# Scores of both attentions: the rounded queries meet the rest of the keys in two 64-row matmuls, one per half of the array

## The chip, the cores and the metric

The kernel runs on one core of one Trainium2 chip. The metric is the time of one execution in microseconds (us), as a median over runs. TensorE (PE) multiplies, VectorE (DVE) and ScalarE (ACT) take its results out of PSUM and round them, GpSimd (POOL) does a few small sums, SyncE (SP) issues the transfers. Each engine works through its own list in order.

## The reference, cut to what matters

One decoder block over 1024 positions, all in float32: a SwiGLU half-step, a mixer of two attentions, a cross attention over 256 memory rows, a second SwiGLU half-step, a final norm. The change is in the mixer's two attentions:

```python
qg = q.reshape(b, s, G, J, D) * (D ** -0.5)          # NSA: 8 heads of width 64, in 2 key groups
s_c = einsum(qg, kc) + bias_c                         # scores against 63 compressed keys
sc  = einsum(qb, kg) + bias                           # against the selected blocks of keys
s_w = einsum(qw, kwin) + bias_w                       # against a window of 512 keys
...
sc = jnp.einsum('bhqd,bkhd->bhqk', qi, k).astype(jnp.float32) + ci[..., None] - c[:, :, None, :]   # FoX: 8 heads
p = masked_softmax(sc, mask)
```

With 16 blocks of 64 keys and top 16 of them, the selection keeps every block up to the query's own, so that the kernel computes it as plain causal attention.

## The kernel before, in words

Matmuls take fp32r operands, which are rounded. To keep float32's precision, each operand is split into a rounded value ("hi") and the rest that rounding left ("lo"). Scores have a contraction of only 64 (the head's width), half of the array's 128 rows, and the kernel uses the other half for the split: a query tile `Q[e]` has the rounded queries in 64 of its rows and their rest in the other 64; a key tile `K1` has the rounded keys twice, one above the other, and `K2` has the rest of the keys twice. So `Q` by `K1` gives (hi + lo) by the rounded keys in one 128-row matmul, and `Q` by `K2` gives (hi + lo) by the rest of the keys in another, accumulated in the same PSUM bank.

`group` (line 1142) does one row of blocks: two heads `e` of NSA for one block of 128 queries, or two neighbouring blocks of queries of one head of FoX. `nb[e]` is the number of 128-key blocks that a row needs. A row that is too wide for one bank of 512 columns is cut into two pieces. For each `e` and each piece, one operation on PE, `scores`, takes a PSUM bank of the tag `s` and issues the matmul by `K1` (line 1167), the one by `K2` (line 1168) and, in the last piece of a window row, one by the 63 compressed keys in plain float32 (line 1170), which the hardware does as two. The weights of all of these, the stationary operand, are the 128 columns of `Q[e]`. Behind them DVE adds bias and mask and takes the minimum (lines 1178, 1265), ACT takes the exponential (line 1195), DVE or ACT scales (1209, 1211), PE transposes the probabilities into tag `T` (line 388), ACT and DVE split them (397, 404), and PE multiplies by the values into tag `pv` (line 1242).

`attention` calls `group` 16 times for each of 4 pairs of NSA heads (8 blocks of queries, each once for the selection and once for the window with the compressed keys) and 4 times for each of 8 FoX heads. Beside these run the projections of the FoX queries, keys and values and of the gates (`proj`, `mm3`, lines 382 to 384, matmuls of 512 columns). `load_q` (line 666) fills `Q` for NSA from DRAM, `proj_q` (line 1075) fills it for FoX from a projection's bank; both write the rounded value and the rest with one ACT and one DVE operation for each `e` and half. `hi_at` says in which 64 rows the rounded queries stand.

The order on every engine is written ahead by a planner (`Plan.order`), a list scheduler with a cost in ns for each operation; it hands out the 8 banks of PSUM, with a cap for each tag (`s` 3, `T` 2, `pv` 1, `mm` 3). An operation on PE gets its banks when it is placed.

Earlier, at line 988, one small product stands in the first SwiGLU: the table of relative biases, a plain float32 matmul with a contraction of 32 and a stationary operand of 8 columns. It is the only place of the kernel where a matmul uses fewer than 128 rows of the array.

Of the kernel before, what the change touches and what calls it, by code (L numbers as in the profile page):

```python
# [10 lines left out]
F32 = mybir.dt.float32  # L11
F32R = mybir.dt.float32r
BF16 = mybir.dt.bfloat16
AF = mybir.ActivationFunctionType
# [5 lines left out]
P = 128  # L20
# [141 lines left out]
class Plan:  # L162
# [120 lines left out]
}  # L283
# [3 lines left out]
class Halves:  # L287
# [13 lines left out]
    def at(self, hf, k, a=0, b=512):  # L301
        return [self.t[hf][s][k // 2]()[:, (k % 2) * 512 + a:(k % 2) * 512 + b] for s in range(2)]
# [19 lines left out]
class Block:  # L322
# [37 lines left out]
    def pe(self, ns, run, reads, writes):  # L360
        self.plan.op({"PE": ns}, lambda _: run(), reads, writes, self.r)
        self.r += ns * self.rate / 1000
# [300 lines left out]
            self.split(1024, lambda raw=raw: [raw()], lambda e=e: [K1[e]()], lambda e=e: [K2[e]()], [raw], [K1[e]], [K2[e]],  # L663
                       rank=r, sbuf=True)

    def load_q(self, name, Q, hi_at, lead=14.0):

        nc = self.nc
        for e in range(2):
            raw, r = self.load_rows(name, e, lead)  # L670
            lo = slice(64 - hi_at[e], 128 - hi_at[e])
            self.act(1024, lambda raw=raw, e=e: nc.scalar.activation(Q[e](), raw(), AF.Copy, scale=-0.125), [raw], [Q[e]],
                     sbuf=True, rank=r)
            self.dve(1135, lambda raw=raw, e=e, lo=lo: nc.vector.scalar_tensor_tensor(
                Q[e]()[lo, :], raw()[lo, :], -0.125, Q[e]()[lo, :].bitcast(F32), op0=ALU.mult, op1=ALU.subtract),
                [raw], [Q[e]], rank=r)
# [395 lines left out]
        self.cd = self.dram([8, S], "cd")  # L1072
        self.dma(32768, lambda: nc.sync.dma_start(self.cd().rearrange("h (b p) -> (h b) p", p=P), ct()[0:64, 0:P]), [ct], [self.cd])

    def proj_q(self, key, hT, Q, hi_at, **k):

        def evac(hf, ps):
            sl = slice(hf * 512, hf * 512 + 512)
            for e in range(2):
                h0 = hi_at[e]  # L1080
                self.split(512, lambda e=e: [ps()[64 * e:64 * e + 64, :]], lambda e=e, h0=h0: [Q[e]()[h0:h0 + 64, sl]],
                           lambda e=e, h0=h0: [Q[e]()[64 - h0:128 - h0, sl]], [ps], [(Q[e], hf)], [(Q[e], hf)], scale=-0.125)
        self.proj(key, hT, evac, **k)

    def proj_k(self, key, hT, K1, K2, **k):
# [56 lines left out]
    def group(self, kind, i, nb, r, Q, K1, K2, V, bias, out, unit, last=True, k0=0, mask=None, cmp=None, gate=None):  # L1142
        nc = self.nc
        mm = nc.tensor.matmul
        rank = self.r
        pe = lambda ns, run, reads, writes: self.plan.op({"PE": ns}, lambda _: run(), reads, writes, rank)
        keys = lambda bs, b: [(x, h) for x in bs for h in range((b + 3) // 4)]
        p, m, l = [self.buf("p") for _ in range(2)], [self.buf("sm") for _ in range(2)], self.buf("sm")
        total = 0.0
        row = [nb[e] * P for e in range(2)]  # L1150
        z = lambda e: p[e]()[:, 896:960]
        for e in range(2):
            n = nb[e]
            if n <= (3 if cmp else 4):
                pieces = [(0, n)]
            else:
                a = min(4, n - 2)
                pieces = [(0, a), (a, n - a)]
            for j, (b, w) in enumerate(pieces):
                end = j == len(pieces) - 1  # L1160
                st = self.buf("s")

                def scores(e=e, b=b, w=w, end=end, st=st):
                    q = Q[e]()[:, i[e] * P:(i[e] + 1) * P]
                    c = max(2, w) * P
                    ks = slice((k0 + b) * P, (k0 + b) * P + c)
                    mm(st()[:, 0:c], q, K1()[:, ks], start=True, stop=False)  # L1167
                    mm(st()[:, 0:c], q, K2()[:, ks], start=False, stop=True)  # L1168
                    if cmp and end:
                        mm(st()[:, 448:512], q.bitcast(F32), cmp[0](), start=True, stop=True)  # L1170
                ns = 2 * max(w * P, 256) / 2.4 + 27 + (110 if cmp and end else 0)
                total += ns
                pe(ns, scores, keys([K1, K2], k0 + b + max(2, w)) + [(Q[e], i[e] // 4)] + ([cmp[0]] if cmp else []), [st])

                if mask is not None and (end if kind == "fox" else j == 0):
                    def masked(w=w, st=st):
                        d = st()[:, w * P - P:w * P] if kind == "fox" else st()[:, 0:P]
                        nc.vector.tensor_add(d, d, mask)
                    self.dve(200, masked, [], [st], rank)

                def biased(e=e, b=b, w=w, j=j, st=st):
                    at = b * P if kind == "fox" else S - row[e] + b * P
                    self.ttr_min(p[e]()[:, b * P:(b + w) * P], st()[:, 0:w * P], bias[e]()[:, at:at + w * P],
                                 m[e]()[:, j - 1:j] if j else 3.0e38, m[e]()[:, j:j + 1])
                self.dve(1.042 * w * P + 74, biased, [bias[e], st] + ([(m[e], j - 1)] if j else []), [(p[e], j), (m[e], j)], rank)
                if end and cmp:
                    def blocks(e=e, st=st):
                        w0 = e * P + 56 - 8 * i[e]
                        self.ttr_min(z(e), st()[:, 448:512], cmp[1]()[:, w0:w0 + 64], 3.0e38, m[e]()[:, 2:3])
                    self.dve(143, blocks, [cmp[1], st], [(p[e], "z"), (m[e], 2)], rank)  # L1190

                    self.pool(90, lambda e=e: nc.gpsimd.memset(p[e]()[:, 960:1024], 0.0), [(m[e], 2)], [(p[e], "end")], rank)

            def exps(e=e, j=len(pieces) - 1):
                nc.scalar.activation(p[e]()[:, 0:row[e]], p[e]()[:, 0:row[e]], AF.Exp, bias=m[e]()[:, j:j + 1], scale=-1.0,  # L1195
                                     accum_out=l()[:, e:e + 1])
                if cmp:
                    nc.scalar.activation(z(e), z(e), AF.Exp, bias=m[e]()[:, 2:3], scale=-1.0, accum_out=l()[:, 2 + e:3 + e])
            self.act(row[e] + (220 if cmp else 70), exps, [m[e]], [p[e], (l, e)], count=4 if cmp else 2, sbuf=True, acc=2 if cmp else 1,
                     table="exp", rank=rank)  # L1200

        k = 4 if cmp else 2
        self.dve(100, lambda: nc.vector.reciprocal(l()[:, 0:k], l()[:, 0:k]), [], [l], rank)
# [14 lines left out]
        n = max(nb)  # L1218
# [57 lines left out]
    def attention(self, hT, kcs, Q, K, V):  # L1276
# [10 lines left out]
        def fox_set(j):  # L1287
            s = dict(Q=u("Q"), K1=u("K1"), K2=u("K2"), V=u("V"))
            return s, [lambda: self.proj_k(("kf", j), hT, s["K1"], s["K2"]), lambda: self.proj_v(("vf", j), hT, s["V"]),
                       lambda: self.proj_q(("qf", j), hT, s["Q"], (0, 64))]  # L1290

        def finish(c, oc):
            if c == 7:
# [6 lines left out]
        for c in range(4):  # L1300
            r0 = self.r
            bias, be = [self.buf("b") for _ in range(2)], self.buf("be")
            self.r = r0 - 6
            self.bias_tile(c, bias, be)
            if c < 3:
                Qn, h0, work = u("Q"), 64 * ((c + 1) // 2), []
                self.r = r0 + 45.0
                self.load_q(("qn", c + 1), Qn, (h0, h0))
                self.r = r0
            else:  # L1310
                fox, work = fox_set(0)
            work += gate(GATES[c])
            r1 = r0 + 51.0 + 10.9 * len(work)
            self.r, self.rate = r0, (r1 - r0) / 51.0
            oc, g, h = self.buf("oc"), c // 2, 2 * c
            for i in range(NT):
                k0, unit = max(0, i - 4), {}
                com = dict(kind="nsa", i=(i, i), r=64 * g, Q=Q, unit=unit, bias=bias, out=(oc, i))
                self.group(nb=(i + 1, i + 1), K1=K[0][0][g], K2=K[0][1][g], V=V[0][g], last=False,
                           gate=lambda i=i, h=h: self.gate()[:, i, 8 + h:10 + h], **com)  # L1320
                self.group(nb=(i + 1 - k0,) * 2, K1=K[1][0][g], K2=K[1][1][g], V=V[1][g], k0=k0, mask=self.win if i >= 4 else None,
                           cmp=(kcs[0][g], be, kcs[1][g]),
                           gate=lambda i=i, h=h: self.gate()[:, i, :].rearrange("p (k h) -> p k h", h=8)[:, 2::-2, h:h + 2], **com)
            self.rate = 1.0
            finish(c, oc)
            self.side(r0, r1, work)
            if c < 3:
                Q = Qn
# [210 lines left out]
    def run(self):  # L1539
# [64 lines left out]
        chains[1]()  # L1604
        for n, k in zip(("ks", "kw"), K):
            self.load_k((n, 0), *k)
        self.load_q(("qn", 0), Q, (0, 0))
        for _ in range(G0):
            self.proj_gate(self.gates.pop(0), hT2)
        self.attention(hT2, self.compressed, Q, K, V)  # L1610
# [28 lines left out]
MLATE = {3: 14.0, 4: 18.0, 1: 24.0, 6: 28.0, 7: 32.0}  # L1639
FIRST = 2  # L1640
G0, AHEAD, MAHEAD, NB = 0, 2, 2, 0
LATER = {4: 8.0, 2: 11.0, 1: 14.0, 6: 17.0, 7: 20.0}


# [20 lines left out]
```

## Time and profile before

| | us |
|---|---|
| median of 3 runs (2528.48 to 2533.14) | 2530.29 |
| the profiled execution | 2531.05 |
| its span, first to last instruction | 2529.3 |
| PE busy | 2497.9 |
| DVE busy | 1777.8 |
| ACT busy | 1201.9 |

How to read it: a matmul's end is modelled and lies well after the start of the next one, since matmuls are pipelined. What a matmul costs PE is therefore read from the distance of two starts. PEld is the load of a matmul's weights into the array, which can run beside the matmul before it. The scores lie between 874 and 1506 us of the span.

### The profile page before, as it was taken

The numbers are of one execution on the slowest core, as the hardware profiler recorded it, in microseconds if no ns is written. First come the engines' busy times: TensorE is split into PE (matmuls) and PEld (weight loads), VectorE is DVE, ScalarE is ACT, GpSimd is POOL, SyncE is SP. The second block draws the span as 40 slices with busy tenths as digits, with TensorE's granted clock in tenths as the row PEclk, the third lists the DMA queues.
The fourth block names the chain that finished last, engine by engine and source line by source line (L and its number), as shares of the span: only waits on it lengthen the run. The fifth ranks groups of instructions, "written<-read, shape, count | busy, mean of one in ns | idle before, by whom it ended". The sixth has DMA issues, their size and how long they took to land.

```text
span 2529.3 us, 34843 instructions
## 1 busy us (share of the span) xinstructions
PE 2497.9 (99%) x12577; PEld 2114.7 (84%) x12577; DVE 1777.8 (70%) x3517; ACT 1201.9 (48%) x2413; POOL 154.9 (6%) x300
## 2 busy tenths in 40 slices
PE   7999999999999999999999999999999999999998
PEld 7888888888888889898888888888888888888887
DVE  8676767776885787788877776343568666667666
ACT  7333232343463677687777853233444223223433
POOL 3000000000000011111010013000010000000001
PEclk9999999999999999999999999999999999999999
DMA  8364224696825612311112244241223323329864
GB/s 311 104 217 137 104 94 158 226 358 235 278 95 155 193 34 80 93 43 45 59 57 78 92 151 158 75 150 53 73 92 113 108 92 112 125 88 321 302 236 168
DMA packets 150317, 358.21 MB, mean 142 GB/s; under 512 B 15968, under 2 KB 23504, under 8 KB 150016
## 3 DMA queue, kind: packets, MB, share of 16 engines
q1 hardware_dynamic: 150080, 355.79, 40.8%
q8 instruction: 99, 1.62, 0.3%
q14 instruction: 74, 0.61, 0.1%
q0 software_dynamic: 64, 0.20, 0.0%
HBM read 274.09 MB, written 83.41 MB: 141 GB/s over the span
## 4 chain that ended last, share of the span: by engine, by line
PE 90%; DVE 5%; ACT 2%; DMA 2%; issue 1%; POOL 0%; SPq 0%; DVEq 0%; POOLq 0%; ACTq 0%
PE z L382 11%; PE z L384 11%; PE z L383 11%; PE mm L382 7%; PE mm L383 7%; PE mm L384 7%; PE y L382 5%; PE y L383 5%; PE y L384 5%; PE T L388 5%; PE pv L1242 4%; PE acc L383 2%; PE acc L384 2%; PE acc L382 2%; PE s L1167 2%; PE s L1168 2%
## 5 line engine op out<-in xcount | busy, mean ns | idle before, releaser
L382 PE MATMUL z<-F,wf 128*128 128x512 f32 x1316 | 512.9, 390 | 1.8 <-ACT t L629 1.1
L384 PE MATMUL z<-F,wf 128*128 128x512 f32 x1316 | 512.1, 389 | 0.3 <-DVE wf L518 0.3
L383 PE MATMUL z<-F,wf 128*128 128x512 f32 x1316 | 512.1, 389 | 0.0
L382 PEld LDWEIGHTS z<-F,wf 128*128 128x128 f32 x1316 | 247.0, 188 | 55.9 <-ACT t L629 1.5
L384 PEld LDWEIGHTS z<-F,wf 128*128 128x128 f32 x1316 | 247.0, 188 | 51.9 <-DVE wf L518 0.7
L383 PEld LDWEIGHTS z<-F,wf 128*128 128x128 f32 x1316 | 247.0, 188 | 51.1
L382 PE MATMUL y<-df,gf 128*128 128x512 f32 x616 | 240.0, 390 | 0.0
L383 PE MATMUL y<-df,gf 128*128 128x512 f32 x616 | 239.7, 389 | 0.0
L384 PE MATMUL y<-df,gf 128*128 128x512 f32 x616 | 239.7, 389 | 0.0
L518 DVE TENSOR_TENSOR wf<-ws,wf 128x512 fp32r<-128x512 f32 x235 | 160.7, 685 | 75.1 <-ACT wf L517 75.0
L404 DVE TENSOR_TENSOR pt<-T,pt 128x512 fp32r<-128x512 f32 (+1 forms) x264 | 154.9, 613 | 51.5 <-ACT pt L397 49.1
L517 ACT CAST wf<-ws 128x512 fp32r<-128x512 f32 x235 | 142.7, 619 | 97.0 <-PE z L384 48.1
L397 ACT CAST pt<-T 128x512 fp32r<-128x512 f32 (+1 forms) x264 | 130.7, 527 | 70.9 <-PE T L388 65.7
L1195 ACT ACTIVATE p<-p,sm 128x128 f32<-128x128 f32 (+7 forms) x192 | 144.1, 751 | 36.4 <-DVE sm L1265 35.0
L495 DVE TENSOR_TENSOR ws<-wa 128x512 f32<-128x512 f32 x235 | 156.5, 683 | 1.8 <-DMA wa<-in_w_dram 1.4
L382 PE MATMUL mm<-h,w 128*128 128x512 f32 x368 | 150.4, 409 | 0.0
L1242 PE MATMUL pv<-pt,V 128*128 128x256 f32 x848 | 142.2, 292 | 2.7 <-DVE pt L404 1.6
L384 PE MATMUL mm<-h,w 128*128 128x512 f32 x368 | 144.2, 392 | 0.0
L383 PE MATMUL mm<-h,w 128*128 128x512 f32 x368 | 144.1, 392 | 0.0
L384 PEld LDWEIGHTS y<-df,gf 128*128 128x128 f32 x616 | 115.6, 188 | 24.2
L382 PEld LDWEIGHTS y<-df,gf 128*128 128x128 f32 x616 | 115.6, 188 | 23.9
L383 PEld LDWEIGHTS y<-df,gf 128*128 128x128 f32 x616 | 115.6, 188 | 23.6
(273 smaller groups left out, 5123.4 us busy)
## 6 DMA issues: line engine op xcount, KB each, us to landing
da<-in_w_dram SPq DMA_DIRECT2D x264, 256.0 KB, 6.0
wa<-in_w_dram SPq DMA_DIRECT2D x104, 512.0 KB, 4.3
wr<-in_w_dram SPq DMA_DIRECT2D x89, 512.0 KB, 4.8
dg<-gd SPq DMA_DIRECT2D x70, 512.0 KB, 6.3
gd<-gs SPq DMA_DIRECT2D x110, 256.0 KB, 2.2
xd<-x SPq DMA_DIRECT2D x24, 512.0 KB, 2.6
x<-xd SPq DMA_DIRECT2D x24, 512.0 KB, 5.8
gd<-sg SPq DMA_DIRECT2D x44, 256.0 KB, 2.2
```

What stands on the lines that cost most here:

```text
L382: mm(out, a[0], b[0], start=first, stop=False, skip_group_check=more)
L383: mm(out, a[0], b[1], start=False, stop=False, skip_group_check=more)
L384: mm(out, a[1], b[0], start=False, stop=last, skip_group_check=more)
L388: self.nc.tensor.transpose(out, src, self.ident[0:k, 0:k])
L397: nc.scalar.copy(h, s)
L404: nc.vector.tensor_sub(l, s, h.bitcast(F32))
L495: self.dve(1.04 * n + 70, lambda: nc.vector.tensor_tensor(out(), a(), b(), op=op), reads, writes, rank)
L517: self.act(512, lambda: nc.scalar.copy(w()[:, 0:512], val()), rd, [(w, 0)], sbuf=True, rank=rank + 3)
L518: self.dve(603, lambda: nc.vector.tensor_sub(w()[:, 512:1024], val(), w()[:, 0:512].bitcast(F32)), rd + [(w, 0)], [(w, 1)], rank=rank + 3)
L1167: mm(st()[:, 0:c], q, K1()[:, ks], start=True, stop=False)
L1195: nc.scalar.activation(p[e]()[:, 0:row[e]], p[e]()[:, 0:row[e]], AF.Exp, bias=m[e]()[:, j:j + 1], scale=-1.0, accum_out=l()[:, e:e + 1])
L1242: mm(pv()[:, 0:256], v, y()[:, b * 256:b * 256 + 256], start=unit["fresh"], stop=stop and y is lo)
```

## The change

- `scores` becomes one operation for both `e` of a piece, with two banks of the tag `s`. It issues, for each `e`, the product by the compressed keys where there is one (now first, and opening the bank), and the 128-row matmul by `K1`; and then, for each `e`, a matmul by `K2` in which only 64 rows take part: for `e` = 0 the rows 0 to 63, for `e` = 1 the rows 64 to 127. These 64 rows hold the rounded queries. The product of the rest of the queries by the rest of the keys is left out.
- For this the rounded queries stand in rows 0 to 63 for `e` = 0 and in rows 64 to 127 for `e` = 1, in every row of work. For NSA `load_q` puts them there by `e`. For FoX both `e` read the same `Q` tile at different blocks, so `proj_q` writes even and odd blocks of 128 queries into opposite halves: two operations of 64x256 in place of one of 64x512, on ACT and on DVE.
- Both `e` share the cuts: a row of six blocks is cut into 3 and 3 (before 4 and 2; and 3 and 2 for its partner of five).
- The cap of the tag `s` goes from 3 to 4 banks. The planner charges an operation both 128-row matmuls, the wider of the two halves and a constant `TURN` of 60 ns.

The core of the diff:

```diff
-    "s": ("ps", 3), "T": ("ps", 2), "pv": ("ps", 1), "mm": ("ps", 3), "acc": ("ps", 4),
+    "s": ("ps", 4), "T": ("ps", 2), "pv": ("ps", 1), "mm": ("ps", 3), "acc": ("ps", 4),
...
-            lo = slice(64 - hi_at[e], 128 - hi_at[e])
+            lo = slice(64 - 64 * e, 128 - 64 * e)
...
-                self.split(512, lambda e=e: [ps()[64 * e:64 * e + 64, :]], lambda e=e, h0=h0: [Q[e]()[h0:h0 + 64, sl]],
-                           lambda e=e, h0=h0: [Q[e]()[64 - h0:128 - h0, sl]], [ps], [(Q[e], hf)], [(Q[e], hf)], scale=-0.125)
+                def at(first, e=e):
+                    return [turns(Q[e]()[r:r + 64, hf * 512:hf * 512 + 512])[a] for a, r in ((0, 64 - first), (1, first))]
+                self.split(512, lambda e=e: turns(ps()[64 * e:64 * e + 64, :]), lambda at=at: at(64), lambda at=at: at(0),
+                           [ps], [(Q[e], hf)], [(Q[e], hf)], scale=-0.125, count=2)
...
-                    mm(st()[:, 0:c], q, K1()[:, ks], start=True, stop=False)
-                    mm(st()[:, 0:c], q, K2()[:, ks], start=False, stop=True)
-                    if cmp and end:
-                        mm(st()[:, 448:512], q.bitcast(F32), cmp[0](), start=True, stop=True)
-                ns = 2 * max(w * P, 256) / 2.4 + 27 + (110 if cmp and end else 0)
...
+        n = max(nb)
+        a = n if n <= (3 if cmp else 4) else n // 2 if n == 6 else min(4, n - 2)
+        cuts = [(0, a)] + [(a, n)] * (a < n)
+        for j, (b, top) in enumerate(cuts):
+            end = j == len(cuts) - 1
+            w = [min(top, nb[e]) - b for e in range(2)]
+            st = [self.buf("s") for _ in range(2)]
...
+                for e in range(2):
+                    c, q = max(2, w[e]) * P, Q[e]()[:, i[e] * P:(i[e] + 1) * P]
                     if cmp and end:
+                        mm(st[e]()[:, 448:512], q.bitcast(F32), cmp[0](), start=True, stop=True)
+                    mm(st[e]()[:, 0:c], q, K1()[:, (k0 + b) * P:(k0 + b) * P + c], start=not (cmp and end), stop=False,
+                       skip_group_check=bool(cmp))
+                for e in range(2):
+                    c, half = max(2, w[e]) * P, slice(64 * e, 64 * e + 64)
+                    mm(st[e]()[:, 0:c], Q[e]()[half, i[e] * P:(i[e] + 1) * P], K2()[half, (k0 + b) * P:(k0 + b) * P + c],
+                       start=False, stop=True, skip_group_check=bool(cmp))
+            cost = [max(x * P, 256) / 2.4 + 13 for x in w]
+            ns = sum(cost) + max(cost) + TURN + (220 if cmp and end else 0)
...
+TURN = 60.0
```

## Rows read from the trace of the kernel before

**Rows 1.** The page of the profiled execution: the span, part 1 (busy time, share of the span, number of instructions of each engine), the granted clock of TensorE in tenths over 40 slices, and part 4 (the chain of work that ended last, by engine).

```profile
span 2529.3 us, 34843 instructions
...
PE 2497.9 (99%) x12577; PEld 2114.7 (84%) x12577; DVE 1777.8 (70%) x3517; ACT 1201.9 (48%) x2413; POOL 154.9 (6%) x300
...
PEclk9999999999999999999999999999999999999999
...
PE 90%; DVE 5%; ACT 2%; DMA 2%; issue 1%; POOL 0%; SPq 0%; DVEq 0%; POOLq 0%; ACTq 0%
```

**Rows 2.** Busy time by stretch, NSA (874 to 1265 us) and FoX (1265 to 1520 us): for PE, PEld, DVE, ACT and POOL the busy us and, after x, the number of instructions; then the granted clock, the DMA share and GB/s.

```profile
874.00:1265.00 391.00, 389.19 (x2486) 347.79 (x2485) 321.84 (x1112) 296.72 (x750) 42.54 (x142) 1.00 0.19 60
1265.00:1520.00 255.00, 251.70 (x1456) 217.28 (x1455) 191.85 (x468) 184.36 (x369) 25.95 (x33) 1.00 0.28 96
```

**Rows 3.** Groups of instructions by line, each shape apart, PE alone: the transposes of the probabilities (L388) and the score matmuls by `K2` (L1168); those by `K1` (L1167) have the same counts. Tile names, rows times columns of the weights, rows times streamed columns, count, busy us and mean ns of one.

```profile
L388 PE MATMUL T<-ident,p 128*128 128x128 f32 x880 | 133.6, 273 | 1.1 <-DVE p L1211 0.8 <-ACT p L1209 0.2
...
L1168 PE MATMUL s<-K,Q 128*128 128x256 f32 x128 | 35.4, 282 | 0.5 <-DVE K L404 0.5
...
L1168 PE MATMUL s<-K,Q 128*128 128x512 f32 x80 | 31.5, 394 | 0.0
L1168 PE MATMUL s<-K,Q 128*128 128x384 f32 x88 | 29.7, 337 | 0.0
```

**Rows 4.** The timeline of PE from 1505 us, in the last row of FoX: start, duration, line, tiles, shape, count.

```profile
1504.81 0.34 PE L1168 MATMUL s<-K,Q 128*128 128x384 f32 x1
1504.99 0.39 PE L1167 MATMUL s<-K,Q 128*128 128x512 f32 x1
...
1505.45 0.64 PE L1242 MATMUL pv<-pt,V 128*128 128x256 f32 x4
1505.92 0.40 PE L1167 MATMUL s<-K,Q 128*128 128x512 f32 x1
...
1506.39 0.39 PE L382 MATMUL mm<-o,w 128*128 128x512 f32 x1
...
1510.47 0.39 PE L382 MATMUL mm<-o,w 128*128 128x512 f32 x1
```

**Rows 5.** The timeline of the weight loads (PEld) at 1051 us: the load for a score matmul in the middle of a row of them.

```profile
1051.11 0.19 PEld L1168 LDWEIGHTS s<-K,Q 128*128 128x128 f32 x1
```

**Rows 6.** The timeline of PE from 1051 to 1054 us: that matmul, and scores behind transposes.

```profile
1051.33 0.39 PE L1168 MATMUL s<-K,Q 128*128 128x512 f32 x1
...
1052.47 1.03 PE L388 MATMUL T<-ident,p 128*128 128x128 f32 x8
1053.26 0.48 PE L1167 MATMUL s<-K,Q 128*128 128x512 f32 x1
1053.58 0.40 PE L1168 MATMUL s<-K,Q 128*128 128x512 f32 x1
```

**Rows 7.** The timeline of PE around the only product with fewer than 128 rows (L988, done as two matmuls of 32 rows).

```profile
425.20 0.39 PE L384 MATMUL z<-F,wf 128*128 128x512 f32 x1
425.52 0.81 PE L988 MATMUL mm<-cs 32*8 32x384 f32 x2
426.26 0.50 PE L382 MATMUL z<-F,wf 128*128 128x512 f32 x1
426.59 0.40 PE L383 MATMUL z<-F,wf 128*128 128x512 f32 x1
```

**Rows 8.** The timeline of PE from 426.3 us, which shows the second of the two matmuls of L988 by itself.

```profile
425.85 0.48 PE L988 MATMUL mm<-cs 32*8 32x384 f32 x1
```

**Rows 9.** The timeline of the weight loads (PEld) around them; in brackets the idle time before a load.

```profile
425.52 0.09 PEld L988 LDWEIGHTS mm<-cs 32*8 32x8 f32 x2 [0.35 <-issue]
426.26 0.19 PEld L382 LDWEIGHTS z<-F,wf 128*128 128x128 f32 x1 [0.65 <-issue]
426.36 0.19 PEld L383 LDWEIGHTS z<-F,wf 128*128 128x128 f32 x1
```

**Rows 10.** The timeline of PE at 853 us, where weights of 64 columns, with all 128 rows, follow weights of 128 columns.

```profile
852.86 0.30 PE L383 MATMUL mm<-w,h 128*128 128x288 f32 x1
852.99 0.29 PE L384 MATMUL mm<-w,h 128*128 128x288 f32 x1
853.12 0.22 PE L382 MATMUL mm<-cs 128*64 128x128 f32 x1
853.18 0.22 PE L383 MATMUL mm<-cs 128*64 128x128 f32 x1
```

**Rows 11.** The timeline of PE at 874 us, where plain float32 (L1170, two matmuls), with all 128 rows, stands between matmuls of fp32r.

```profile
874.31 0.28 PE L1168 MATMUL s<-K,Q 128*128 128x256 f32 x1
874.43 0.33 PE L1170 MATMUL s<-kcc,Q 128*128 128x64 f32 x2
874.58 0.36 PE L1167 MATMUL s<-K,Q 128*128 128x256 f32 x1
```

**Rows 12.** Of the instructions that touch the tile `Q`, those that fill it for FoX: count, duration in ns (least, median, most), first and last start.

```profile
L399 ACT ACTIVATE Q<-mm x16: 589/592/598, 1221.0 to 1445.6; 64x512 fp32r<-64x512 f32 x16
L406 DVE SCALAR_TENSOR_TENSOR Q<-mm,Q x16: 683/688/694, 1223.2 to 1446.9; 64x512 fp32r<-64x512 f32 x16
```

More of the change, by code (lines that the diff above doesn't have):

```diff
@@ L664, in load_k, with load_q @@
                        rank=r, sbuf=True)
-    def load_q(self, name, Q, hi_at, lead=14.0):
+    def load_q(self, name, Q, lead=14.0):
         nc = self.nc
@@ L1073, in forget, with proj_q @@
         self.dma(32768, lambda: nc.sync.dma_start(self.cd().rearrange("h (b p) -> (h b) p", p=P), ct()[0:64, 0:P]), [ct], [self.cd])
-    def proj_q(self, key, hT, Q, hi_at, **k):
+    def proj_q(self, key, hT, Q, **k):
         def evac(hf, ps):
-            sl = slice(hf * 512, hf * 512 + 512)
+            turns = lambda t: [t.rearrange("p (b two t) -> p two b t", two=2, t=P)[:, a] for a in range(2)]
             for e in range(2):
-                h0 = hi_at[e]
-                self.split(512, lambda e=e: [ps()[64 * e:64 * e + 64, :]], lambda e=e, h0=h0: [Q[e]()[h0:h0 + 64, sl]],
-                           lambda e=e, h0=h0: [Q[e]()[64 - h0:128 - h0, sl]], [ps], [(Q[e], hf)], [(Q[e], hf)], scale=-0.125)
+                def at(first, e=e):
+                    return [turns(Q[e]()[r:r + 64, hf * 512:hf * 512 + 512])[a] for a, r in ((0, 64 - first), (1, first))]
+                self.split(512, lambda e=e: turns(ps()[64 * e:64 * e + 64, :]), lambda at=at: at(64), lambda at=at: at(0),
+                           [ps], [(Q[e], hf)], [(Q[e], hf)], scale=-0.125, count=2)
         self.proj(key, hT, evac, **k)
@@ L1151, in group @@
         z = lambda e: p[e]()[:, 896:960]
[L1152 to L1166, printed above, removed]
-                    mm(st()[:, 0:c], q, K1()[:, ks], start=True, stop=False)
-                    mm(st()[:, 0:c], q, K2()[:, ks], start=False, stop=True)
-                    if cmp and end:
-                        mm(st()[:, 448:512], q.bitcast(F32), cmp[0](), start=True, stop=True)
-                ns = 2 * max(w * P, 256) / 2.4 + 27 + (110 if cmp and end else 0)
-                total += ns
-                pe(ns, scores, keys([K1, K2], k0 + b + max(2, w)) + [(Q[e], i[e] // 4)] + ([cmp[0]] if cmp else []), [st])
+        n = max(nb)
@@ new lines, in group, with scores @@
+        a = n if n <= (3 if cmp else 4) else n // 2 if n == 6 else min(4, n - 2)
[4 more added lines that the diff above has]
+            st = [self.buf("s") for _ in range(2)]
+            def scores(b=b, w=w, end=end, st=st):
+                for e in range(2):
+                    c, q = max(2, w[e]) * P, Q[e]()[:, i[e] * P:(i[e] + 1) * P]
+                    if cmp and end:
+                        mm(st[e]()[:, 448:512], q.bitcast(F32), cmp[0](), start=True, stop=True)
[7 more added lines that the diff above has]
+            ns = sum(cost) + max(cost) + TURN + (220 if cmp and end else 0)
+            total += ns
+            pe(ns, scores, keys([K1, K2], k0 + b + max(2, max(w))) + [(Q[e], i[e] // 4) for e in range(2)] + ([cmp[0]] if cmp else []), st)
+            for e in range(2):
@@ L1175, in group, with masked @@
                 if mask is not None and (end if kind == "fox" else j == 0):
-                    def masked(w=w, st=st):
-                        d = st()[:, w * P - P:w * P] if kind == "fox" else st()[:, 0:P]
+                    def masked(x=w[e], st=st[e]):
+                        d = st()[:, x * P - P:x * P] if kind == "fox" else st()[:, 0:P]
                         nc.vector.tensor_add(d, d, mask)
-                    self.dve(200, masked, [], [st], rank)
-                def biased(e=e, b=b, w=w, j=j, st=st):
+                    self.dve(200, masked, [], [st[e]], rank)
@@ L1182, in biased @@
+                def biased(e=e, b=b, x=w[e], j=j, st=st[e]):
                     at = b * P if kind == "fox" else S - row[e] + b * P
-                    self.ttr_min(p[e]()[:, b * P:(b + w) * P], st()[:, 0:w * P], bias[e]()[:, at:at + w * P],
+                    self.ttr_min(p[e]()[:, b * P:(b + x) * P], st()[:, 0:x * P], bias[e]()[:, at:at + x * P],
                                  m[e]()[:, j - 1:j] if j else 3.0e38, m[e]()[:, j:j + 1])
-                self.dve(1.042 * w * P + 74, biased, [bias[e], st] + ([(m[e], j - 1)] if j else []), [(p[e], j), (m[e], j)], rank)
@@ L1186, in group, with blocks @@
-                if end and cmp:
-                    def blocks(e=e, st=st):
+                self.dve(1.042 * w[e] * P + 74, biased, [bias[e], st[e]] + ([(m[e], j - 1)] if j else []), [(p[e], j), (m[e], j)], rank)
+                if not end:
+                    continue
+                if cmp:
+                    def blocks(e=e, st=st[e]):
                         w0 = e * P + 56 - 8 * i[e]
                         self.ttr_min(z(e), st()[:, 448:512], cmp[1]()[:, w0:w0 + 64], 3.0e38, m[e]()[:, 2:3])
-                    self.dve(143, blocks, [cmp[1], st], [(p[e], "z"), (m[e], 2)], rank)
+                    self.dve(143, blocks, [cmp[1], st[e]], [(p[e], "z"), (m[e], 2)], rank)
@@ L1192, in group @@
                     self.pool(90, lambda e=e: nc.gpsimd.memset(p[e]()[:, 960:1024], 0.0), [(m[e], 2)], [(p[e], "end")], rank)
[L1194 to L1198, printed above, removed]
@@ L1199, in group, with exps @@
-            self.act(row[e] + (220 if cmp else 70), exps, [m[e]], [p[e], (l, e)], count=4 if cmp else 2, sbuf=True, acc=2 if cmp else 1,
-                     table="exp", rank=rank)
+                def exps(e=e, j=j):
+                    nc.scalar.activation(p[e]()[:, 0:row[e]], p[e]()[:, 0:row[e]], AF.Exp, bias=m[e]()[:, j:j + 1], scale=-1.0,
+                                         accum_out=l()[:, e:e + 1])
+                    if cmp:
+                        nc.scalar.activation(z(e), z(e), AF.Exp, bias=m[e]()[:, 2:3], scale=-1.0, accum_out=l()[:, 2 + e:3 + e])
@@ L1202, in group @@
+                self.act(row[e] + (220 if cmp else 70), exps, [m[e]], [p[e], (l, e)], count=4 if cmp else 2, sbuf=True,
+                         acc=2 if cmp else 1, table="exp", rank=rank)
         k = 4 if cmp else 2
@@ L1289, in fox_set @@
             return s, [lambda: self.proj_k(("kf", j), hT, s["K1"], s["K2"]), lambda: self.proj_v(("vf", j), hT, s["V"]),
-                       lambda: self.proj_q(("qf", j), hT, s["Q"], (0, 64))]
+                       lambda: self.proj_q(("qf", j), hT, s["Q"])]
         def finish(c, oc):
@@ L1305, in attention @@
             if c < 3:
-                Qn, h0, work = u("Q"), 64 * ((c + 1) // 2), []
+                Qn, work = u("Q"), []
                 self.r = r0 + 45.0
-                self.load_q(("qn", c + 1), Qn, (h0, h0))
+                self.load_q(("qn", c + 1), Qn)
                 self.r = r0
@@ L1606, in run @@
             self.load_k((n, 0), *k)
-        self.load_q(("qn", 0), Q, (0, 0))
+        self.load_q(("qn", 0), Q)
         for _ in range(G0):
```

## The prediction

> **What bounds the kernel now.** I read the page first: PE is busy 99% of the span and holds 90% of the chain that ended last, and its granted clock is full in every slice, 2.4 GHz of the two levels [rows 1]. So a nanosecond of PE is a nanosecond of the kernel, unless the stage that changes is another engine's. The windows of that stage answer: in NSA and FoX together PE is busy 640.9 of 646 us, DVE 513.7, ACT 481.1 [rows 2]. PE is the bound there too, with 5.1 us idle. A busy PE could still hide waits, since a matmul's modelled end lies beyond the next one's start. So I read starts: in the last row of FoX matmuls of 512 columns start every 0.227 us (18 steps from 1506.39 to 1510.47), four of 256 columns take 0.47, so 0.118 each, and one of 384 takes 0.18, which I set at 0.173, midway between the other two [rows 4]. Nothing waits between them. The loads of their weights cost nothing, for each runs beside the matmul before: the load for the matmul of 1051.33 starts at 1051.11 [rows 5, 6]. The list is dense, and the change must be priced in starts, not in busy time.
>
> **What goes.** The matmuls by `K2` are 128 of 256 columns, 88 of 384 and 80 of 512 [rows 3], which is 128 x 0.118 + 88 x 0.173 + 80 x 0.227 = 48.5 us of PE. In the new kernel two of them share the array. Counting from the code's cuts: a pair of NSA heads has 25 operations, 11 of 256 columns, 10 of 384, 4 of 512; a FoX head has 6, whose wider halves are one of 256, two of 384, three of 512. Four pairs and eight heads make 148 operations: 52, 56 and 40. If the two halves stream at the same time, this takes 52 x 0.118 + 56 x 0.173 + 40 x 0.227 = 24.9 us. Gone: **23.6 us**, or 0.16 us for each operation. The matmuls by `K1` keep their columns (the new cuts 3 + 3 only move them), and those by the compressed keys only come earlier in their operation.
>
> **What comes: two turns of the array in each operation.** Each operation now goes from 128 rows to 64 and back. The trace has no matmul of 64 rows, but it has one product of 32 [rows 7 to 9], and I take the price from it, step by step. The last full matmul starts at 425.20 and would let the next start at 425.43; the first narrow one starts at 425.52: 0.09 us late. Its weights weren't loaded ahead: their load starts at 425.52 too, and the row says that PEld stood idle before it and waited for nothing that shows. The second narrow one starts at 425.85, 0.33 behind the first; the full one behind it could start at 426.18 and its load starts at 426.26: 0.08 late. This load too wasn't made ahead, and so the matmul stands for it: it lasts 0.50 where 0.39 is usual, and the next one starts 0.33 behind it, not 0.23. That is 0.10 to 0.11. Together 0.09 + 0.08 + 0.11 = **0.28 us** for there and back.
>
> Is it the rows? Two neighbours say so. Weights of 64 columns with all 128 rows follow weights of 128 columns without a gap: starts at 852.86, 852.99, 853.12 [rows 10]. And plain float32 between fp32r starts 0.12 behind its predecessor, as usual; behind it a load lies partly open, because 64 streamed columns are too short to cover it, but nothing waits for the array [rows 11]. So neither the type nor the columns make PE wait; the rows are what is left, though this product changed both at once.
>
> To that the weights of the halves must be added. Those at 425.52 had 8 columns and both loads took 0.09 by their modelled ends; a half has 128. What 128 columns take is shown by the matmul of 426.26 (0.11) and by the transposes: eight of them take 1.03 with the last one's 0.27, so 0.109 each [rows 3, 6], though 128 columns stream in 0.06 [rows 10]. Transposes start at the pace of their loads, which come one after another. So the first half waits 0.11 for its weights, and the second, whose load follows, starts another 0.11 later. The sum of a turn is 0.28 + 0.11 + 0.11 = **0.50 us**, in 148 operations 74.0 us. The operation behind has its own first load in the open; that is the 0.11 already counted. Scores that follow transposes stand for part of a load today as well (0.48 in place of 0.39 at 1053.26 [rows 6]), but that is the load by `K1`, which stays.
>
> Both ends of this unknown: at the low end there is no wait at all for 64 rows, with loads ahead as today, 0 us, which leaves a gain. At the high end the halves don't stream together: then nothing is saved, the second half's load is covered by the first, and 0.39 us a turn are added, 57.7 us. I take 0.50 with halves side by side, because the row of 32 is the nearest, and both of its turns say the same.
>
> The Trainium skill, TensorE: Matmul & The Clock Gate, Part 3 (The mechanism), has it that loads for another row group are pulled ahead of running matmuls, and that matmuls of different row groups start about 4 ns apart. By this the second half's load would cost nothing: a rival below. On the turn itself the skill's TensorEngine Tiling (Array Packing), Key Properties, says that a change of the tiling mode drains the engine, and that a change of tile alone doesn't; by it 64 rows behave as the 32 here did, which no run here shows.
>
> **What costs nothing or little.** The 16 evacuations into `Q` for FoX, 593 ns on ACT and 688 on DVE [rows 12], become two each; even if each half cost as much as the whole that is 16 x 0.59 = 9.4 us of ACT and 11 of DVE over a stage in which they have 165 and 132 us free [rows 2]. Uncovered it would be those 9 to 11 us; PE hides it. The operation waits for two free banks and for both `Q` tiles, and behind it in PE's list stand transposes, value products and projections. All that PE waits for in the stage now is 5.1 us [rows 2]; one bank more of tag `s` against two taken at a time from the same eight may double it or halve it: +5 to -3 us, taken as 0. A slower PE leaves DVE and ACT more time, so this is small in the forecast case. No transfer is added or moved.
>
> **The sum.** 2531.05 (profiled) - 23.6 + 74.0 = 2581.4 us; the median of the runs is 0.8 us below the profiled execution, so **2580.7 us**, 2.0% slower.
>
> **Rivals.**
> 1. *The halves' loads run side by side.* The turn is then 0.28 + 0.11 = 0.39: 57.7 - 23.6 = +34 us, 2564. For it: the two loads go to different halves of the array. Against it: the pace of the transposes, though these load the same rows. With both loads hidden it is 0.28: +17.8, 2548.
> 2. *The two halves run one after the other*, so that the change doesn't do what it says: +57.7, 2588.
> 3. *Turning to half the rows needs no drain* (faster). Then loads go ahead, and at most one stands open, the second half's: 148 x 0.11 - 23.6 = -7.3, so 2523; with none open 2507. For it: the product of 32 rows changed rows and columns together and happened once, and a wait that the profile can't see could lie in its way in. Against it: the way back lost as much. It decides at 0.16 us a turn: below that the change gains.
> 4. *A turn of about that price*, as two drains of 0.08 with every load hidden: -23.6 + 25.2, no change, 2531.
>
> **How the numbers follow.** The forecast's own sort, a turn of 0.28 us or more, has 0.72: both loads in a row 0.40, side by side or hidden 0.19, halves in a row 0.13; by itself it spans 2545 to 2592 with the banks' 3 to 5 us. Rival 4 has 0.08, rival 3 has 0.20. About 0.2%, 5 us, is what a measurement of this kernel can tell from no change. So slower 0.72, same 0.08, faster 0.20. The range goes to 2592 at the top, and at the bottom to 2520, which takes in rival 4 and the dearer half of rival 3; the rest of that rival, about 0.1, and 0.03 at the top stay outside.
>
> **What would show it.** In the changed kernel's timeline of PE, the first half's load starts some 0.09 us after the `K1` matmul has streamed, not beside it; the second half starts 0.11 behind the first; the next operation's first load starts 0.08 behind the end of the stream, and its matmul is recorded 0.11 longer. Scores with their turns take 50 us more of the stage between 874 and 1506, and no other stage moves. If instead the loads of the halves lie beside the `K1` matmuls, rival 3 holds; if the halves start a full stream apart, rival 2. I'd be wrong altogether if PE's waits for banks or for DVE grew by tens of us, or if the granted clock fell in the stage.

## The result, and the profile after

| | us | against before |
|---|---|---|
| before, median of 4 runs | 2529.59 | |
| changed, median of 4 runs (2558.14 to 2560.86) | 2559.55 | ratio 1.0116, 95% interval 1.0098 to 1.0133 |
| span of the profiled execution, before and after | 2529.3 and 2556.4 | +27.1 |

The change makes the kernel 1.2% slower, some 30 us. The forecast was 2580.7 in a range of 2520 to 2592: the sign and the mechanism held, the size was 21 us too large. One of the eleven runs of a kernel below, the one with halves for 512 columns alone, took 6494.43 us, far beyond all others, and is left out of its numbers.

The page of the changed kernel, to be laid beside [rows 1]: span, part 1, the granted clock and the chain by engine.

```profile
span 2556.4 us, 34880 instructions
...
PE 2530.4 (99%) x12577; PEld 2099.1 (82%) x12577; DVE 1782.7 (70%) x3537; ACT 1204.9 (47%) x2425; POOL 143.8 (6%) x300
...
PEclk9999999999999999999999999999999999999999
...
PE 93%; DVE 3%; ACT 2%; DMA 1%; issue 1%; POOL 0%; SPq 0%; DVEq 0%; POOLq 0%; ACTq 0%
```

PE has the same 12577 matmuls, and is as busy in its share as before; the clock is full. Busy time alone doesn't tell what happened. The weight loads give a hint: they are busy 16 us less in a longer span, though no load was taken away, so some of them now lie side by side.

Where the time lies is read from a landmark that both kernels have, the first matmul of the output projection (all instructions on the tile `acc`; count, ns, first and last start). First the kernel before, then the changed one:

```profile
L382 PE MATMUL acc<-w,h x256: 387/389/481, 1562.5 to 1888.6; 128*128 128x512 f32 x128
```

```profile
L382 PE MATMUL acc<-w,h x256: 388/389/478, 1590.4 to 1916.3; 128*128 128x512 f32 x128
```

It starts 27.9 us later. The first score starts at 874.2 before and 874.1 after, and from the landmark to the end they differ by less than a microsecond (966.8 and 966.0 us). All of the loss is in the stage with the two attentions.

The same two stretches as in [rows 2], FoX ending later now (PE, PEld, DVE, ACT, POOL busy, granted clock, DMA share, GB/s):

```profile
874.00:1265.00 391.00, 390.60 (x2363) 319.76 (x2363) 304.97 (x1064) 284.38 (x719) 40.82 (x138) 1.00 0.16 50
1265.00:1545.00 280.00, 278.46 (x1566) 224.66 (x1565) 209.49 (x530) 198.69 (x415) 26.29 (x37) 1.00 0.29 98
```

PE stands idle 1.9 of 671 us, where it was 5.1 of 646: PE is still the bound, and waits a little less for the others. The same NSA stretch holds 2363 matmuls where it held 2486.

The timeline of PE around one operation at 1103 us, with 256 columns; the second fence shows the second `K1` matmul by itself, the third the weight loads:

```profile
1102.85 0.60 PE L388 MATMUL T<-ident,p 128*128 128x128 f32 x4
1103.20 0.48 PE L1168 MATMUL s<-K,Q 128*128 128x256 f32 x2
1103.61 0.38 PE L1172 MATMUL s<-K,Q 64*128 64x256 f32 x2
1103.93 0.50 PE L382 MATMUL mm<-F,w 128*128 128x512 f32 x1
1104.27 0.40 PE L383 MATMUL mm<-F,w 128*128 128x512 f32 x1
1104.51 0.40 PE L384 MATMUL mm<-F,w 128*128 128x512 f32 x1
```

```profile
1103.40 0.28 PE L1168 MATMUL s<-K,Q 128*128 128x256 f32 x1
```

```profile
1103.61 0.19 PEld L1172 LDWEIGHTS s<-K,Q 64*128 64x128 f32 x2
1103.93 0.19 PEld L382 LDWEIGHTS mm<-F,w 128*128 128x128 f32 x1
1104.04 0.19 PEld L383 LDWEIGHTS mm<-F,w 128*128 128x128 f32 x1
```

Read it from start to start. The `K1` matmul of 1103.40 has 256 columns, 0.12 us; the halves start at 1103.61, 0.09 late. Their loads start with them, not ahead. Two halves together last 0.38 and their two loads 0.19: both run at the same time. By the trace's nanoseconds the second half starts 3 or 4 ns behind the first in each of the 148 operations. From 1103.61 to the next start are 0.32, of which 0.12 is the stream: the other 0.20 is the halves' load (0.11) and the wait on the way out (0.09). The projection's load at 1103.93 lies in the open too: its matmul lasts 0.50 and the next starts 0.34 behind, 0.11 more than the 0.23 of [rows 4]. A turn is 0.09 + 0.11 + 0.09 + 0.11 = 0.40; over all 148 operations the trace's medians are 0.096, 0.200 for the two in the middle, and 0.107, within 0.02 of the 0.39 that the account below goes on with.

### The profile page after: what moved, and what is told of

Same layout as the page of the kernel before. It is cut to its first block, busy times and chain, and to the rows that moved or that the text cites. A ratio compares the mean times of both kernels' runs of the same rounds, so it can differ in the third digit from the quotient of the medians.

```text
span 2556.4 us, 34880 instructions
## 1 busy us (share of the span) xinstructions
PE 2530.4 (99%) x12577; PEld 2099.1 (82%) x12577; DVE 1782.7 (70%) x3537; ACT 1204.9 (47%) x2425; POOL 143.8 (6%) x300
## 4 chain that ended last, share of the span: by engine, by line
PE 93%; DVE 3%; ACT 2%; DMA 1%; issue 1%; POOL 0%; SPq 0%; DVEq 0%; POOLq 0%; ACTq 0%
PE z L382 11%; PE z L383 11%; PE z L384 11%; PE mm L382 8%; PE mm L383 7%; PE mm L384 7%; PE y L383 5%; PE y L384 5%; PE y L382 5%; PE T L388 5%; PE pv L1248 4%; PE acc L383 2%; PE acc L382 2%; PE acc L384 2%; PE s L1168 2%; PE s L1172 2%
## 5 line engine op out<-in xcount | busy, mean ns | idle before, releaser
L517 ACT CAST wf<-ws 128x512 fp32r<-128x512 f32 x235 | 142.8, 620 | 97.5 <-PE z L384 48.5
```

The lines of the kernel that those rows point to most:

```text
L517: self.act(512, lambda: nc.scalar.copy(w()[:, 0:512], val()), rd, [(w, 0)], sbuf=True, rank=rank + 3)
```

## The experiments

Theory A: each turn of the array to 64 rows and back costs PE 0.39 us, made up as above; the halves stream side by side, which gives back 0.16 us an operation. Rival B: the new arrangement costs (two banks at once, common cuts, evacuations in turns), and the narrow matmuls are cheap. Rival C: the planner's charge of 60 ns for a turn spoils the order. Rival D: the price is per 64-row pair, not per turn.

| kernel | turns | us | ratio to before, 95% interval |
|---|---|---|---|
| changed | 148 | 2559.55 | 1.0116 (1.0098 to 1.0133) |
| all rows full | 0 | 2529.28 | 0.9996 (0.9986 to 1.0005) |
| no matmuls by K2 | 0 | 2503.82 | 0.9896 (0.9881 to 0.9911) |
| both in the same half | 148 | 2580.38 | 1.0198 (1.0183 to 1.0214) |
| halves twice | 148 | 2581.25 | 1.0201 (1.0184 to 1.0218) |
| charge of 300 ns | 148 | 2567.86 | 1.0144 (1.0127 to 1.0161) |
| one turn a row | 96 | 2610.84 | 1.0316 (1.0301 to 1.0332) |
| one half, one full | 148 | 2579.42 | 1.0192 (1.0177 to 1.0208) |
| two turns | 296 | 2636.14 | 1.0419 (1.0403 to 1.0435) |
| halves for 512 columns alone | 40 | 2534.97 | 1.0019 (1.0010 to 1.0028) |

All but "charge of 300 ns" and "one turn a row" keep the order of the changed kernel on every engine outside the score operations.

**All rows full.**

```diff
-                    c, half = max(2, w[e]) * P, slice(64 * e, 64 * e + 64)
+                    c, half = max(2, w[e]) * P, slice(0, P)
```

> The changed kernel with its order, cuts, banks and Q layout, but both matmuls by K2 take all 128 rows, as before the change (rounded queries and their rest by the rest of the keys). Theory A (each turn of the array costs 0.39 us: 0.09 wait in, 0.11 load of the halves, 0.09 wait out, 0.11 load of the next; streams side by side give 0.16 back): 148 x 0.23 = 34 us below the changed kernel, 2525 to 2531 us. Rival B (the new arrangement costs: two banks at once, common cuts, evacuation in turns; the narrow matmuls are cheap): stays near 2559, or rises by the 23 us of streams.

It gives the time of before. Order, cuts, banks and the layout of `Q` cost nothing that shows: rival B falls, and the 30 us hang on the 64 rows alone.

**No matmuls by K2.**

```diff
-                    mm(st[e]()[:, 0:c], q, K1()[:, (k0 + b) * P:(k0 + b) * P + c], start=not (cmp and end), stop=False,
+                    mm(st[e]()[:, 0:c], q, K1()[:, (k0 + b) * P:(k0 + b) * P + c], start=not (cmp and end), stop=True,
...
-                for e in range(2):
-                    c, half = max(2, w[e]) * P, slice(64 * e, 64 * e + 64)
-                    mm(st[e]()[:, 0:c], Q[e]()[half, i[e] * P:(i[e] + 1) * P], K2()[half, (k0 + b) * P:(k0 + b) * P + c],
-                       start=False, stop=True, skip_group_check=bool(cmp))
```

> The changed kernel without the matmuls by K2 (the rounded queries by the rest of the keys are left out). Theory A: a turn and its streams go, 148 x 0.39 + 25 = 83 us less, 2477 us, up to 15 us more where DVE and ACT become the bound of the stage. Rival B: only the 25 us of streams go, 2535.

2503.8, which is 56 us below the changed kernel, between the two expectations. Against the kernel with all rows full 48.5 us of streams went and only 25.5 came back. In this kernel PE waits, by the list of waits between 870 and 1480 us (engine, line, who released it; us, times, longest):

```profile
PE pv L1244 <- DVE pt L404: 5.6, 17, 0.7
PE T L388 <- DVE p L1213: 1.6, 4, 0.7
PE mm L383 <- DVE o L404: 1.0, 1, 1.0
```

Waits shorter than the overlap of a matmul's modelled end don't appear in it, so these rows are a lower bound. The starts of PE's matmuls show more. Summed up to the landmark, where a start came later than its predecessor's stream or load explains and a semaphore of DVE or ACT had just let it go, it is some 27 us in this kernel and some 8 with all rows full: about 20 of the missing 23 us are waits for DVE and ACT. What this suggests for the change: even a free turn might not have given all of the 23.6 us back, though no kernel here saves just that.

**Both in the same half.**

```diff
-            lo = slice(64 - 64 * e, 128 - 64 * e)
+            lo = slice(64, 128)
...
-                    return [turns(Q[e]()[r:r + 64, hf * 512:hf * 512 + 512])[a] for a, r in ((0, 64 - first), (1, first))]
+                    return [turns(Q[e]()[r:r + 64, hf * 512:hf * 512 + 512])[a] for a, r in ((0, 64 - first), (1, 64 - first))]
...
-                    c, half = max(2, w[e]) * P, slice(64 * e, 64 * e + 64)
+                    c, half = max(2, w[e]) * P, slice(0, 64)
```

> The changed kernel with the rounded queries in rows 0 to 63 for both e, so that both 64-row matmuls of an operation use the same half of the array. Theory A (the two halves do stream at the same time, and their loads are made together): they now stream one after the other, +23 us, 2583; the second load is hidden under the first stream. If the halves were not at the same time in the changed kernel: no change, 2560.

+20.8 us. The halves of the changed kernel do run at the same time; here two take 0.43 from the first's start to the next matmul, there 0.32. The timeline of PE at 952 us, then the loads: the second half's load takes its own time behind the first's (0.29 for two, where the changed kernel's two took 0.19).

```profile
952.11 0.50 PE L1172 MATMUL s<-K,Q 64*128 64x256 f32 x2
952.54 0.44 PE L388 MATMUL T<-ident,p 128*128 128x128 f32 x2
```

```profile
952.11 0.29 PEld L1172 LDWEIGHTS s<-K,Q 64*128 64x128 f32 x2
```

**Halves twice.**

```diff
-                for e in range(2):
+                for n, e in enumerate((0, 1, 0, 1)):
...
-                       start=False, stop=True, skip_group_check=bool(cmp))
+                       start=False, stop=n > 1, skip_group_check=bool(cmp))
```

> The changed kernel with the pair of 64-row matmuls issued twice in each operation (the rest of the keys counts double). Theory A (the price is the turn, paid once; inside the 64-row mode loads run ahead and both halves' loads go side by side): + 148 streams, +25 us, 2585. Rival D (the price is per 64-row pair, loads in the open or one behind the other inside the mode as well): +25 and 148 x 0.11 to 0.22 more, 2600 to 2617.

+21.7 us, no more than the streams: rival D falls. Four halves at 912.61 and the next matmul; then their loads:

```profile
912.61 0.50 PE L1172 MATMUL s<-K,Q 64*128 64x256 f32 x4
913.05 0.50 PE L1248 MATMUL pv<-pt,V 128*128 128x256 f32 x2
```

```profile
912.61 0.30 PEld L1172 LDWEIGHTS s<-K,Q 64*128 64x128 f32 x4
```

Four halves take 0.44 from start to start, where two took 0.32: one more stream of 0.12. Inside the narrow mode the second pair's loads run beside the first pair's streams, as loads do everywhere else in the kernel. Only the turn stops them.

**One half, one full.**

```diff
-                for e in range(2):
-                    c, half = max(2, w[e]) * P, slice(64 * e, 64 * e + 64)
+                for e in (1, 0):
+                    c, half = max(2, w[e]) * P, slice(0, P if e else 64)
```

> The changed kernel's order, but of the two matmuls by K2 that of e = 1 takes all 128 rows and only that of e = 0, behind it, takes 64 rows. So each operation turns once, and nothing streams beside anything. Theory A (the turn alone costs 0.39 us): 148 x 0.39 = 58 us above the kernel with all rows full (2529), 2587. If part of the price belonged to two halves at work at once: 2560 to 2580.

2579.4, +50.1 us over all rows full, 0.34 us a turn. That is 8 us below theory A's 2587 and inside the other range, in which part of the price belonged to two halves at work at once. The starts decide: over all 148 turns of this kernel the medians are 0.09 on the way in, 0.19 for the half's load and the way out, and 0.11 for the next load, 0.39 together, next to 0.40 with two halves. So one half alone pays the whole turn, and the 8 us are not missing from the turn itself; where such differences lie is told below. The loads at 1039 us, in order: that of the full matmul runs ahead, that of the half after it stands behind 0.25 us of idle time for which nothing is named, and the next full one (L1167) behind 0.18 more.

```profile
1039.31 0.19 PEld L1172 LDWEIGHTS s<-K,Q 128*128 128x128 f32 x1
1039.74 0.18 PEld L1172 LDWEIGHTS s<-K,Q 64*128 64x128 f32 x1 [0.25 <-issue]
1040.11 0.30 PEld L1167 LDWEIGHTS s<-kcc,Q 128*128 128x128 f32 x2 [0.18 <-issue]
```

**Two turns.**

```diff
                 for e in range(2):
                     c, q = max(2, w[e]) * P, Q[e]()[:, i[e] * P:(i[e] + 1) * P]
...
                        skip_group_check=bool(cmp))
-                for e in range(2):
                     c, half = max(2, w[e]) * P, slice(64 * e, 64 * e + 64)
```

> The changed kernel with its matmuls in another order inside an operation: K1 of e = 0, its half by K2, K1 of e = 1, its half. Two turns in each operation and nothing side by side. Theory A (a turn costs 0.39 us, 0.34 net of the waits that it makes vanish, as with one half full): 296 turns, 2529 + 296 x 0.34 to 0.39 = 2630 to 2645, if the granted clock holds; more if the drained array lets it fall to 1.2 GHz as in the kernel with one turn a row. If the price were per operation and not per turn: 2580.

2636.1, within theory A's range: 106.9 us over all rows full, 0.36 a turn, again with nothing side by side. The price goes by the turn and not by the operation.

**Halves for 512 columns alone.**

```diff
-                    c, half = max(2, w[e]) * P, slice(64 * e, 64 * e + 64)
+                    c, half = max(2, w[e]) * P, slice(64 * e, 64 * e + 64) if max(w) == 4 else slice(0, P)
```

> The changed kernel with halves only in the 40 operations whose wider piece has 512 columns; the 108 others take full 128 rows by K2 (as with all rows full, 2529). Theory A: 40 x (0.39 - 0.23) = 6 us above 2529, 2535: even at the widest bank a turn doesn't pay. If a turn cost less than 0.23 us: at or below 2529.

2535.0, 5.7 us over all rows full: slower even where a turn saves most, 0.227 us. No bank of scores is wide enough for it.

**Charge of 300 ns.**

```diff
-TURN = 60.0
+TURN = 300.0
```

> The changed kernel with the planner's charge for a turn at 300 ns in place of 60, near what the trace shows (0.39 us); the same instructions, in the order that this charge gives. Theory A (PE is the bound and its list dense whatever the order): within 4 us of the changed kernel, 2556 to 2564. Rival C (an order planned on too cheap a turn costs): 10 us or more below, 2545.

2567.9, outside theory A's range, and to the other side than rival C has it: the order that was planned on the truer price is 8 us slower than that planned on 60 ns. So the planner's charge isn't the cause. PE waited a little more in this order, 1.7 us at 979 for DVE, and from there its clock was granted at half for 6.8 us (window, PE, PEld, DVE, ACT, POOL, granted clock, DMA share, GB/s):

```profile
966.00:979.90 13.90, 12.07 (x75) 9.53 (x73) 6.86 (x27) 6.95 (x18) 2.61 (x11) 1.00 0.62 143
979.90:986.70 6.80, 6.65 (x24) 5.51 (x25) 2.67 (x14) 2.44 (x8) 0.00 (x0) 0.50 0.00 0
1563.60:1567.00 3.40, 3.40 (x10) 2.62 (x9) 1.98 (x3) 0.97 (x2) 2.51 (x2) 0.50 0.46 145
```

That costs about 3.4 us, and the second such stretch, the last line, 1.7. From the first score to the landmark (872.0 to 1601.5 us) this execution takes 13.1 us longer than the changed kernel's, for the same matmuls. PE stands idle 7.3 us in it, where it was 1.9; these 5.4 us of waits and the 5.1 of clock make 10.5 of the 13.1, and the rest was not settled. So theory A was wrong that PE's list is dense whatever the order: the order decides how much PE waits.

**One turn a row.** All pieces of a row become one operation, which also holds the buffers for the probabilities from then on; the `K1` matmuls of all pieces come first:

```diff
+        sts = [[self.buf("s") for _ in range(2)] for _ in cuts]
+        def scores():
+            for j, (b, top) in enumerate(cuts):
...
+            for j, (b, top) in enumerate(cuts):
+                w, st = ws[j], sts[j]
                 for e in range(2):
...
+        self.plan.op({"PE": ns}, lambda _: scores(), ..., sum(sts, []), rank, hold=p)
```

> The changed kernel with one operation for a whole row of blocks: all matmuls by K1 of both pieces first, then all halves, in up to four banks; 96 turns in place of 148. Theory A: 52 turns of 0.39 less, -20 us, 2540, with up to 10 us of waits for four banks at once on top: 2540 to 2550. Rival B (banks and arrangement are the cost): no gain, 2560 or more.

2610.8: 52 turns fewer, and 51 us slower. Theory A expected 2540 to 2550, rival B 2560 or more, and there it lies. The two stages, then the three longest waits of PE between 860 and 1600 us:

```profile
874.00:1265.00 391.00, 371.82 (x2139) 307.83 (x2137) 267.91 (x921) 252.21 (x635) 36.40 (x121) 0.96 0.16 51
1265.00:1545.00 280.00, 259.69 (x1478) 213.19 (x1478) 209.78 (x580) 204.23 (x438) 26.26 (x47) 0.95 0.21 70
```

```profile
PE T L388 <- DVE p L1220: 20.8, 15, 3.5
PE pv L1251 <- DVE pt L404: 9.1, 19, 1.2
PE pv L1251 <- ACT pt L397: 7.6, 10, 1.1
```

PE now stands idle 39.5 us in 671, waiting for DVE and ACT, and the granted clock has fallen to 0.96 and 0.95. So this kernel doesn't weigh the turn: with four of the eight banks taken at a time, the rows of blocks no longer overlap enough to cover the softmax between them. That the waits come from the banks is inferred from the waits' order; the buffers that are held for the probabilities could make them as well, and a version with fewer banks and the same turns wasn't tried. So it doesn't speak for rival B, whose two banks at a time cost nothing with all rows full, and it leaves theory A unweighed; the number of turns is weighed by the kernels with 40, 148 and 296 of them.

## Why the prediction was right, and where it was off

**The bound** was right: PE idle 1.9 us of the stage after, and every us in its list counts. **What goes** was right: the halves run together, and giving the second its own stretch costs 20.8 (same half) to 21.7 us (halves twice), where 23.6 to 24.9 was worked out. **The turn** was read from the right rows: 0.09 in, 0.08 out and 0.11 for the next load at the one product of 32 rows [rows 7 to 9] came back as 0.09, 0.09 and 0.11 at 64 rows. Two drains and loads that can't run ahead are the mechanism; the rows, not the columns or the type, set it off, as the neighbours had it [rows 10, 11]. The Trainium skill's TensorEngine Tiling (Array Packing), Key Properties, says that changing the mode drains TensorE and changing only the tile doesn't. The trace agrees: 0.09 us pass unused at each end of a visit, and four halves take 0.44 us against two in 0.32.

**The term that was off is the second half's load**: "the second, whose load follows, starts another 0.11 later". It doesn't follow; both loads are made in the same 0.11, and 148 x 0.11 = 16.3 us of the forecast fall away. I took the pace of the transposes for the pace of all loads, though I noted that these load the same rows; the kernel with both halves in one half of the array shows that this was the difference. That is rival 1, to which I gave 2564, and it was the case, though it had only 0.19 of the chances (loads side by side or hidden) and the forecast's own sum 0.40: the result lies in the range because the range took the rivals in. The Trainium skill's TensorE: Matmul & The Clock Gate, Part 3 (The mechanism), states that matmuls of different row groups start about 4 ns apart. The trace agrees, with 3 or 4 ns between the two halves.

**The second miss is the waits**, which I took as 0 with -3 to +5. With rival 1 the sum is 148 x 0.39 - 23.6 = 34.1 us; measured against all rows full it is 30.3. The pattern repeats: 50.1 for 57.7 (one half), 106.9 for 115.4 (two turns), 5.7 for 6.5 (512 columns alone), 20.8 and 21.7 for 23.6 and 24.9. About a tenth of what is added to PE's list doesn't show. Some of it is in view: a turn in front of transposes (27 of the 148) leaves only 0.06 in the open, since these go at the pace of their loads anyway (four take 0.66 behind a turn, and 0.60 at 1102.85):

```profile
1061.83 0.66 PE L388 MATMUL T<-ident,p 128*128 128x128 f32 x4
```

The whole can be read start by start beside the kernel with all rows full, whose order is the same. Up to the landmark the distances at the turns grow by 56.1 us, 0.38 a turn; less the 23.6 of streams that is 32.5. All other distances shrink by 2.5, most of it at the value products, and 30.0 is left. That they shrink because a slower PE meets fewer waits for DVE and ACT fits the idle time (1.9 us, and 3.0 with all rows full), but wasn't tested by itself.

**Rival 2** (halves in a row) falls with the same-half kernel, **rival 3** (no drain) and **rival 4** (a turn of 0.16) with the timeline and with the kernels of 40, 148 and 296 turns. (The 25.2 us of rival 4 are 0.09 + 0.08 a turn, not two of 0.08.) The evacuations into `Q` cost nothing, by all rows full. The clock, which I had named as what could make me wrong, held in the changed kernel, but not in three that I built from it (charge of 300 ns, one turn a row, two turns).

## What to carry to other kernels

Before packing small contractions side by side in the array, price the turn into that mode and back from any narrow matmul that the trace already has: the wait before it, the wait behind it, and the loads that no longer run ahead. Here that is 0.39 us, so a visit must save more than that in one go; inside the mode, work streams and loads as usual, so more narrow matmuls in a row might pay, which no run here shows, and two of 512 columns don't. And where PE is at 99% with its neighbours at 75 to 80%, a gain on PE is soon capped: taking 48.5 us out of its list gave 25.5.

## What the runs showed that I had not expected

Two weight loads into opposite halves of the array take the time of one, also behind a turn, where neither was made ahead: 0.19 us on the record for two, where two into the same half took 0.29.

The granted clock can fall around PE's waits. In the kernel with one turn a row it falls from 2.4 to 1.2 GHz nine times between 919 and 1323 us. Windows around one of the falls (PE, PEld, DVE, ACT, POOL, granted clock, DMA share, GB/s), and PE's list before it, with its idle time in brackets:

```profile
1258.00:1271.20 13.20, 9.42 (x61) 7.17 (x59) 8.92 (x37) 8.49 (x25) 1.14 (x4) 1.00 0.06 21
1271.20:1278.00 6.80, 5.72 (x23) 4.74 (x23) 3.72 (x13) 4.63 (x9) 0.00 (x0) 0.50 0.00 0
1278.00:1288.30 10.30, 5.95 (x42) 4.67 (x41) 7.81 (x31) 6.45 (x17) 1.14 (x4) 1.00 0.01 2
```

```profile
1267.43 0.38 PE L1251 MATMUL pv<-pt,V 128*128 128x256 f32 x1 [0.57 <-ACT pt L397]
1268.16 0.63 PE L1251 MATMUL pv<-pt,V 128*128 128x256 f32 x3 [0.34 <-DVE pt L404]
1268.62 0.74 PE L1166 MATMUL s<-K,Q 128*128 128x384 f32 x4
1269.30 0.56 PE L1172 MATMUL s<-K,Q 64*128 64x384 f32 x4
1271.82 0.47 PE L388 MATMUL T<-ident,p 128*128 128x128 f32 x1 [1.96 <-DVE p L1220]
```

In the 13.2 us before it fell PE was busy 9.4 by the profile, and it fell within a wait of 1.96 us for DVE. Over the stage a granted clock of 0.96 in 391 us and 0.95 in 280 means some 60 us at half speed (2 x (0.04 x 391 + 0.05 x 280)), which would account for up to 30 of that kernel's 51 us. A wait on PE can so cost more than its own length.

No wait needs to be in view for it. In the kernel with two turns the clock is at half from 937.3 us for 3.4 us. In the 7.3 us before PE shows no idle time; it turned to 64 rows and back six times:

```profile
930.00:937.30 7.30, 7.30 (x29) 4.77 (x29) 6.39 (x24) 5.28 (x13) 0.00 (x0) 1.00 0.07 25
937.30:940.70 3.40, 3.40 (x13) 2.92 (x13) 0.69 (x1) 1.08 (x2) 0.00 (x0) 0.50 0.00 0
```

That the turns brought it down is not shown: the changed kernel turns 148 times at the full clock.
